# Norm weights moved out of the rows that the experts gather, router logits in column groups, residual on VectorE, biases in four transposes

## The chip, the cores and the metric

One core of a Trainium2 chip runs one launch of the program. The metric is the device time of that launch in microseconds. The kernel before took 1209.48 us (median of 3 runs, 1208.46 to 1210.07).

## What is computed

A decoder layer over 256 tokens of 1024 features: a layer norm, a mixer of three groups (a state-space group, sparse attention, memory attention) that one output projection merges, a second layer norm, and a mixture of 32 experts of which each token takes 4. What the change touches, cut from the reference:

```
mix = concat([y_ssd, y_dsa, y_mem], -1) @ w_out[l]
h = layer_norm(ALPHA * h + mix, ln1_g[l], ln1_b[l])
...
logits = h2 @ router_w + router_b
top_val, top_idx = lax.top_k(logits, 4)
gates = softmax(top_val)
...                                    # per expert e, on the tokens that chose it
gu = xb @ w_gu[e] + b_gu[e]
y  = clamped_swiglu(gu) @ w_down[e] + b_down[e]
...
h = layer_norm(ALPHA * h + sum of gates * y, ln2_g[l], ln2_b[l])
```

All data is 32-bit floating point. The weights of the experts are 384 MiB of the 424 MiB (444.75 MB) that are moved.

## The kernel before

The program has two stages. The *trunk* computes everything up to the second norm and the router. The *expert stage* runs through 32 experts, for each eight row blocks of `w_gu` and four of `w_down`, 1 MiB each, loaded once and used once. A token block `tb` is 128 tokens; there are two.

**Buffers and loads.** All weights, of trunk and experts, go through one set of buffers in SBUF. The loads are issued by SyncE (SP) in a fixed order, `load(c)` at line 379, each as soon as its buffer has been given back. Expert weights are therefore loaded while the trunk still computes, as far as the trunk has given buffers back: twenty of them stand in SP's order before the first one that needs a buffer which an expert has used up.

**Order of the work.** Each piece of work is a generator (`g_...`) that says which engine it wants next and how long it expects to hold it. A list scheduler (`run`, line 242) writes the instructions of all engines in one order when the program is built; each engine then runs its own instructions strictly in that order, and waits on semaphores for data of the others. Priorities are given where a task is added (`add(g, prio)`, a lower number first).

**The output projection** (`g_main`, line 1643, name `out`) accumulates `P`, 128 x 1024 in PSUM, for each token block over 16 row blocks of `w_out`. It begins with two matmuls that put `ALPHA * H` into `P`, by a scaled identity `alphaI` (lines 294 and 1670). Eight row blocks use exact 32-bit matmuls on `yhi`; the other eight, with `shi` and `slo`, use three products of operands that are split into a high and a low part (`w`: split on ScalarE and VectorE, lines 1569 and 1582). The last eight row blocks are done for token block 0, then for token block 1.

**Between the projection and the experts** (`g_ln1`, `g_route`, lines 1142 to 1227), for each token block: ScalarE copies `P` to `res`; VectorE takes mean and variance, a reciprocal root in ten small steps (`rsqrt`), and applies the norm with its weights to get `h` (`h1`); TensorE transposes `res` (`tp`), ScalarE copies the transposes (`hT`), TensorE multiplies by the router's weights (`pl`) into 32 rows and transposes back; VectorE makes the logits (`lgr`), picks four (`sel`), TensorE counts positions (`ppos`), VectorE finishes them (`posm`) and the gates. The norm's weights are folded into the router's weights beforehand by `g_fold` (line 529), sixteen matmuls with 32 columns.

**Gathering.** For each pair of experts VectorE builds a one-hot matrix `oh` from `posm`, TensorE multiplies `h` by it (`pg`), ScalarE copies the product to `xg` (line 1306), and `xg` is the stationary operand of the first expert matmul, `P<-raw,xg`. `g_open` (line 1272) lets the experts begin; `g_start` (line 1237) sets the accumulator `H` to `ALPHA * h` plus gates times `b_down`. `g_bias` (line 505) turns `b_gu` round with sixteen transposes from 32 partitions.

`l1` holds `ln1_g` and `ln1_b`, each spread over 128 partitions by a load of 512 KB in the trunk (line 1138).

Of the kernel before, what the change touches and what calls it, by code (L numbers as in the profile page):

```python
# [15 lines left out]
D = 1024  # L16
NE = 32
# [42 lines left out]
def moe_layer(tc, x, mem, ln_in_g, ln_in_b, w_in, conv_w, conv_b, dt_bias, a_log, d_skip, ssd_norm_g,  # L60
# [233 lines left out]
    alphaI = jp  # L294
    V.tensor_scalar(out=alphaI, in0=ident, scalar1=ALPHA, scalar2=None, op0=OP.mult)
# [14 lines left out]
    free["t8"] += [(0.0, (trunk, f"t8x_{i}", 2048)) for i in range(T8 - T8R)]  # L310

# [112 lines left out]
    bgr = t8([NE, 2 * D], "bgr")  # L424
# [78 lines left out]
    gbT = trunk.tile([128, 16], F32, name="gbT")  # L503

    def g_bias():
        yield after("bgr")
        for q in range(2):
            yield "T", 0.5, "mp"
            pv = take("mp", [128, 8, 64], "pbg")
            for f in range(8):  # L510
                o = q * 1024 + f // 2 * 256 + f % 2
                T.transpose(pv[:, f, :NE], bgr[:, o:o + 255:2], ident[:NE, :NE])
            yield "A", 0.4
            A.copy(out=bgT[:, q * 8:q * 8 + 8, :], in_=pv[:, :, :NE])
            give(pv)
# [13 lines left out]
    def g_fold():  # L529

        yield "T", 1.5, "mp"
# [601 lines left out]
    def g_l1():  # L1133
        yield after("dsa00", "dsa01", "dsa10", "dsa11", "mem0", "mem1")
        yield lambda: min((f[0] for f in free["t8"] if f[1][0] is trunk), default=None)
        l1 = t8([128, 2, D], "l1")
        for i, src in enumerate((ln1_g, ln1_b)):
            nc.sync.dma_start(out=l1[:, i, :], in_=_bcast(src, D))
        L1["g"], L1["b"] = l1[:, 0, :], l1[:, 1, :]
        finish_at("l1")  # L1140
# [24 lines left out]

    def g_route(r, tb, mv, rs):
        hT1 = trunk.tile([128, 8, 128], F32, name="hT1", tag=("vtok", "bc")[tb])
        lgr = trunk.tile([128, 40], F32, name="lgr", tag=f"lgr{tb}")
# [11 lines left out]
        yield "T", 1.8, "mp"  # L1180
# [14 lines left out]
        m8 = trunk.tile([128, 8], F32, name="m8r", tag=f"m8r{tb}")  # L1195
        nm = trunk.tile([128, 1], F32, name="nmr", tag=f"nmr{tb}")
# [5 lines left out]
        add(g_gate(lgr, m8, nm, tb), 8)  # L1202
# [6 lines left out]
        mm(p[:, :NE], supper, sel[:, tb, :], start=tb == 0, stop=True)  # L1209
        yield "V", 0.2  # L1210
# [5 lines left out]
    def g_gate(lgr, m8, nm, tb):  # L1216
# [5 lines left out]
        gs = trunk.tile([128, 1], F32, name="gs", tag=f"gs{tb}")  # L1222
# [14 lines left out]
    def g_start():  # L1237
# [9 lines left out]
        bd = take("bd", [NE, D], "bd")  # L1247
        G.dma_start(out=bd, in_=b_down[0])
        yield "W", 8.0
        yield after(LATE)  # L1250
        for tb in range(2):
# [4 lines left out]
            gT = take("sg", [NE, 128], "gT")  # L1256
            A.copy(out=gT, in_=p[:NE, :128])
            give(p)
            for hf in range(2):
# [5 lines left out]
                V.scalar_tensor_tensor(out=H[:, tb, cs], in0=L1["h1"][:, tb, cs], scalar=ALPHA, in1=p, op0=OP.mult,  # L1265
                                       op1=OP.add)
# [4 lines left out]

    def g_open():

        yield after("pos0", "pos1", "h100", "h101", "h110", "h111", "gate0", "gate1")
# [10 lines left out]
        add(g_start(), 9)  # L1285
        add(g_l2())
# [8 lines left out]
    def gather(oh, xg, n, q):  # L1295
# [9 lines left out]
        yield "A", 0.6  # L1305
        A.copy(out=xg[:, :n, q * 4:q * 4 + 4, :], in_=pv[:, :, :n, :].rearrange("p j e s -> p e j s"))  # L1306
# [292 lines left out]
    def begin(name):  # L1599
# [27 lines left out]
        if name == "out":  # L1627
            add(g_l1())
# [14 lines left out]
    def g_main():  # L1643
# [8 lines left out]
        for i, tb in units:  # L1652
# [31 lines left out]
            for j, (w, r) in enumerate(prods):  # L1684
                for c0, d0, wid in wd:
                    mm(Pt[tb][:, d0:d0 + wid], w, r[:, c0:c0 + wid], start=k == 0 and j == 0 and name != "out",
                       stop=last and j == len(prods) - 1)
            if tb:
# [3 lines left out]
                else:  # L1692
                    used_up(c, o)
            if last:
# [3 lines left out]
                if tb and name == "out":  # L1698
                    give(*Y.values())
# [151 lines left out]
```

## Time and profile before

| What | Value |
|---|---|
| Time, median of 3 runs | 1209.48 us |
| Profiled execution, its own time | 1209.03 us |
| Its span, first to last instruction | 1207.2 us |
| TensorE (PE) busy | 1125.4 us, 93% |
| VectorE (DVE) busy | 369.1 us, 31% |
| ScalarE (ACT) busy | 276.2 us, 23% |
| Moved by DMA | 444.75 MB, 368 GB/s over the span |

The span's start is 0 in all times below. The output projection's last matmul starts at 250.7 us, the first expert matmul at 271.2 us. Engines are named PE, PEld (the weight loads of PE), DVE, ACT, POOL and SP as the profile does. An exact 32-bit matmul stands in the trace as two instructions, so that `x16` can be eight matmuls. An operand's buffer number is left out of its name; `two`, `raw` and `w` are weight buffers and scratch.

### The profile page before, as it was taken

How to read it: one execution, taken by the hardware profiler on the slowest of the kernel's cores; microseconds unless marked ns; L12 is line 12 of the kernel's file. 1: busy time of each engine (PE TensorE's matmuls, PEld its weight loads, DVE VectorE, ACT ScalarE, POOL GpSimd, SP SyncE). 2: the span in 40 equal slices, each digit the busy share in tenths (PEclk: the TensorE clock that was granted, in tenths of full speed). 3: DMA queues.
4: the chain of work that ended last, by engine and by line, in shares of the span. 5: the costliest groups of instructions: out<-in, count | busy, mean ns of one | idle time of the engine just before them, and what ended most of it. 6: DMA issues, size and time to landing. Idle time of an engine off the chain costs nothing. (4 is left out here: it accounts for less than half of the span.)

```text
span 1207.2 us, 13744 instructions
## 1 busy us (share of the span) xinstructions
PE 1125.4 (93%) x5491; PEld 536.1 (44%) x5491; DVE 369.1 (31%) x864; ACT 276.2 (23%) x583; POOL 8.4 (1%) x21
## 2 busy tenths in 40 slices
PE   7999999989999999999998989898989898989894
PEld 5777785774343434434343424242424242424231
DVE  6579667751222211212112111212121112111124
ACT  3576894311111111111111111111111111111110
POOL 1000000000000000000000000000000000000000
PEclk9999999989999999999999999999999999999997
DMA  8845345699999999999999999999999999999993
GB/s 282 280 147 201 105 158 226 231 366 375 422 421 422 422 420 422 422 422 421 422 422 422 421 422 421 422 423 420 422 421 422 423 420 423 420 422 422 421 421 139
DMA packets 71653, 444.75 MB, mean 368 GB/s; under 512 B 9669, under 2 KB 11089, under 8 KB 22145
## 3 DMA queue, kind: packets, MB, share of 16 engines
q1 hardware_dynamic: 70896, 441.43, 89.7%
q0 software_dynamic: 688, 2.39, 0.6%
q8 instruction: 45, 0.74, 0.3%
q14 instruction: 24, 0.19, 0.0%
HBM read 442.73 MB, written 1.06 MB: 368 GB/s over the span
## 5 line engine op out<-in xcount | busy, mean ns | idle before, releaser
L80 PE MATMUL P<-raw,xg 128*64 128x512 f32 x2048 | 464.1, 597 | 33.9 <-DMA raw<-in_w_gu_dram 33.8
L80 PEld LDWEIGHTS P<-raw,xg 128*64 128x64 f32 x2048 | 139.1, 136 | 328.3 <-issue 233.3
L80 PE MATMUL P<-raw,aT 128*64 128x512 f32 x1024 | 238.2, 598 | 12.4 <-DMA raw<-in_w_down_dram 11.2
L1370 DVE TENSOR_TENSOR gb<-tp,bgT 128x512 f32<-128x512 f32 x64 | 44.0, 687 | 574.7 <-PE tp L1366 574.7
L80 PEld LDWEIGHTS P<-raw,aT 128*64 128x64 f32 x1024 | 68.8, 136 | 153.7 <-issue 105.0
L1388 ACT COPY ps<-P 128x512 f32<-128x512 f32 x64 | 34.5, 589 | 416.6 <-PE P L80 416.6
L1425 DVE TENSOR_TENSOR H<-H,psc 128x512 f32<-128x512 f32 x68 | 43.7, 684 | 160.0 <-PE psc L80 160.0
L80 PE MATMUL P<-w,hhi 128*128 128x512 f32 (+1 forms) x288 | 82.2, 401 | 2.1 <-DVE w L1582 2.1
L80 PEld LDWEIGHTS pg<-oh,h 128*128 128x128 f32 x512 | 61.8, 197 | 23.6 <-issue 11.4
L80 PE MATMUL pg<-oh,h 128*128 128x128 f32 x512 | 67.9, 288 | 1.3 <-DVE oh L1292 1.3
L80 PE MATMUL psc<-ye,oht 64*128 64x512 f32 x256 | 63.9, 616 | 0.8 <-ACT ye L1430 0.8
L80 PEld LDWEIGHTS P<-w,hhi 128*128 128x128 f32 x288 | 52.3, 189 | 13.4 <-DVE w L1582 3.0
L1430 ACT ACTIVATE ye<-P,oht 128x512 f32<-128x512 f32 x32 | 22.0, 687 | 124.0 <-PE P L80 124.0
L1377 ACT ACTIVATE sg<-gb 128x256 f32<-128x256 f32 x64 | 26.7, 417 | 96.7 <-DVE gb L1373 96.7
L1306 ACT COPY xg<-pg 128x512 f32<-128x512 f32 x32 | 18.7, 586 | 127.9 <-PE pg L80 127.9
L80 PE MATMUL P<-w,hlo 128*128 128x512 f32 (+1 forms) x144 | 45.7, 390 | 0.0
L1366 PEld LDWEIGHTS tp<-ident,ps 128*128 128x128 f32 x256 | 33.2, 209 | 25.2 <-ACT ps L1388 21.9
L1366 PE MATMUL tp<-ident,ps 128*128 128x128 f32 x256 | 39.2, 296 | 0.0
L1582 DVE TENSOR_TENSOR w<-two,w 128x1024 fp32r<-128x1024 f32 (+2 forms) x28 | 31.3, 1135 | 20.1 <-ACT w L1569 19.8
L1582 DVE TENSOR_TENSOR w<-raw,w 128x1024 fp32r<-128x1024 f32 (+2 forms) x28 | 31.6, 1142 | 18.0 <-ACT w L1569 17.3
L80 PEld LDWEIGHTS psc<-ye,oht 64*128 64x128 f32 x256 | 21.9, 186 | 31.1 <-issue 28.4
L1569 ACT CAST w<-raw 128x1024 fp32r<-128x1024 f32 (+2 forms) x28 | 26.9, 982 | 16.6 <-PE P L80 9.3
(295 smaller groups left out, 788.0 us busy)
## 6 DMA issues: line engine op xcount, KB each, us to landing
raw<-in_w_gu_dram SPq DMA_DIRECT2D x256, 1024.0 KB, 19.8
raw<-in_w_down_dram SPq DMA_DIRECT2D x128, 1024.0 KB, 19.8
two<-in_w_in_dram SPq DMA_DIRECT2D x16, 512.0 KB, 3.8
raw<-in_w_in_dram SPq DMA_DIRECT2D x6, 1024.0 KB, 6.5
two<-in_w_out_dram SPq DMA_DIRECT2D x8, 512.0 KB, 4.0
raw<-in_w_out_dram SPq DMA_DIRECT2D x4, 1024.0 KB, 5.4
LT<-scr_d POOLq DMA_DIRECT2D x2, 1024.0 KB, 6.0
two<-in_w_in_dram SPq DMA_DIRECT2D x6, 264.0 KB, 6.5
```

The source lines that it names most:

```text
L80: T.matmul(o, lhsT=l, rhs=r, start=start, stop=stop)
L1306: A.copy(out=xg[:, :n, q * 4:q * 4 + 4, :], in_=pv[:, :, :n, :].rearrange("p j e s -> p e j s"))
L1366: T.transpose(pv[:, f, :], ps[:, o:o + 255:2], ident)
L1370: V.tensor_tensor(out=gb, in0=pv.rearrange("p f (c s) -> p f c s", c=2), in1=bcol(half).to_broadcast([128, 4, 2, SLOTS]), op=OP.add)
L1377: A.activation(out=sg, in_=gb[:, :, 0, :], func=AF.Sigmoid, scale=1.702)
L1388: A.copy(out=ps[:, c * 512:c * 512 + 512], in_=P[:, c * 512:c * 512 + 512])
L1425: V.tensor_tensor(out=H[:, tb, cs], in0=H[:, tb, cs], in1=ps[hf], op=OP.add)
L1430: A.mul(out=ye, in_=Q[:, :512], mul=oht[:, 256:257])
L1569: A.copy(out=parts[i][0][0], in_=raw_of[c][o])
L1582: V.tensor_tensor(out=lo, in0=raw_of[c][o], in1=hi.bitcast(F32), op=OP.subtract)
```

## The change

- `alphaI` and the four matmuls with it go. `g_ln1` makes `res` with `scalar_tensor_tensor` on VectorE, `ALPHA * H + P`, in two halves; the two copies on ScalarE go. The last row block's matmuls are ordered by halves of the columns.
- The norm's weights are no longer applied before the gather: `h1` is `(res - mean) * rs`, made by two `activation` instructions on ScalarE for each token block. The weights go in when `pg` is evacuated to `xg`: four `activation` instructions with per-partition scale and bias in place of one copy.
- The residual's `ln1_g` is multiplied in later by `g_resid`, in the middle of the expert stage, with a load of `ln1_g` spread over partitions; `ln1_b` comes in as a 33rd row of the matmul with `b_down`. The loads of `l1` in the trunk go.
- Router logits: the eight matmuls write to four groups of 32 rows, and a matmul with `four` (four identities on top of one another) adds the groups. Token block 0's routing has priority 5 in place of 8, token block 1's -1 in place of 0.
- `g_fold` does its sums on VectorE and one matmul in place of sixteen.
- `b_gu` is loaded in four parts on 128 partitions and turned by four transposes in place of sixteen.
- `warm(n)` adds matmuls whose results nobody reads: 8 at the start, 9 and 5 in token block 1's routing.
- Gates are no longer waited for by `g_open`, but by `g_back` and by the load of `b_down`.

The diff, cut to its core:

```diff
-    alphaI = jp
-    V.tensor_scalar(out=alphaI, in0=ident, scalar1=ALPHA, scalar2=None, op0=OP.mult)
+    four, fs = jp[:, 0:NE], jp[:, NE:3 * NE].rearrange("p (c e) -> p c e", c=2)
...
+    def warm(n):
+        t = take("mp", [128, 512], "warm")
+        for i in range(n):
+            mm(t[:, i % 4 * 128:i % 4 * 128 + 128], ident, ident)
+        give(t)
+    warm(8)
...
     def g_bias():
-        for q in range(2):
-            for f in range(8):
-                T.transpose(pv[:, f, :NE], bgr[:, o:o + 255:2], ident[:NE, :NE])
+        for f in range(4):
+            T.transpose(pv[:, f, :], bgr[:, o:o + 255:2], ident)
...
     def g_fold():
-        for k in range(8):
-            mm(p[:, :NE], gbT[:, 8 + k:9 + k].to_broadcast([128, 128]), rw[:, k, :], start=k == 0, stop=k == 7)
...
-        for k in range(8):
-            mm(p[:, NE:2 * NE], ones, rw[:, k, :], start=k == 0, stop=k == 7)
+        V.tensor_tensor(out=t, in0=rw, in1=by(gbT[:, 8:16]), op=OP.mult)
+        V.tensor_reduce(out=fs[:, 0, :], in_=t.rearrange("p k e -> p e k"), axis=AX.X, op=OP.add)
+        V.tensor_tensor(out=rw, in0=rw, in1=by(gbT[:, 0:8]), op=OP.mult)
+        V.tensor_reduce(out=fs[:, 1, :], in_=rw.rearrange("p k e -> p e k"), axis=AX.X, op=OP.add)
+        mm(p[:, :2 * NE], ones, jp[:, NE:3 * NE])
...
     def g_ln1(P, tb):
-            A.copy(out=r[:, cs], in_=P[:, cs])
+            V.scalar_tensor_tensor(out=r[:, cs], in0=H[:, tb, cs], scalar=ALPHA, in1=P[:, cs], op0=OP.mult, op1=OP.add)
-        add(g_route(r, tb, mv, rs), 0 if tb else 8)
+        add(g_route(r, tb, mv, rs), -1 if tb else 5)
-        V.scalar_tensor_tensor(out=H[:, tb, :], in0=r, scalar=mv[:, 0:1], in1=L1["g"], op0=OP.subtract, op1=OP.mult)
+        V.tensor_scalar(out=nm, in0=mv[:, 0:1], scalar1=rs, scalar2=-1.0, op0=OP.mult, op1=OP.mult)
-            V.scalar_tensor_tensor(out=L1["h1"][:, tb, cs], in0=H[:, tb, cs], scalar=rs, in1=L1["b"][:, cs], op0=OP.mult,
-                                   op1=OP.add)
+            A.activation(out=L1["h1"][:, tb, cs], in_=r[:, cs], func=AF.Identity, scale=rs, bias=nm)
...
     def g_route(r, tb, mv, rs):
-            mm(pl[:NE, :128], rw[:, k, :], hT1[:, k, :], start=k == 0, stop=k == 7)
+            q = k % 4 * 32
+            mm(pl[q:q + 32, :128], rw[:, k, :], hT1[:, k, :], start=k < 4, stop=k >= 4)
-        T.transpose(pl[:, 256:256 + NE], lgT, ident[:NE, :NE])
+        mm(pl[:, 256:256 + NE], lgT, four)
+        if tb:
+            warm(9)
...
+        if tb:
+            warm(5)
...
+    def g_resid():
+        yield after("start1", "aT201")
+        nc.sync.dma_start(out=g, in_=_bcast(ln1_g, D))
+                V.scalar_tensor_tensor(out=t, in0=L1["h1"][:, tb, cs], scalar=ALPHA, in1=g[:, cs], op0=OP.mult, op1=OP.mult)
+                V.tensor_tensor(out=H[:, tb, cs], in0=H[:, tb, cs], in1=t, op=OP.add)
...
     def gather(oh, xg, n, q):
-        A.copy(out=xg[:, :n, q * 4:q * 4 + 4, :], in_=pv[:, :, :n, :].rearrange("p j e s -> p e j s"))
+        for j in range(4):
+            A.activation(out=xg[:, :n, k, :], in_=pv[:, j, :n, :], func=AF.Identity, scale=gbT[:, k:k + 1],
+                         bias=gbT[:, 8 + k:9 + k])
...
     def g_main():
-                if name == "out":
-                    for c0 in (0, 512):
-                        mm(Pt[tb][:, c0:c0 + 512], alphaI, H[:, tb, c0:c0 + 512], stop=False)
+            if last:
+                steps.sort(key=lambda x: x[1])
```

**What moves on PE, where token block 1's part of the output projection begins.** Before, its row blocks (`P<-w,shi` and `P<-w,slo`, six instructions each) follow one another:

```order
L80 MATMUL P<-w_2556,shi 128x512 x4
L80 MATMUL P<-w_2556,slo 128x512 x2
L80 MATMUL P<-w_2087,shi 128x512 x4
L80 MATMUL P<-w_2087,slo 128x512 x2
L80 MATMUL P<-w_2115,shi 128x512 x4
L80 MATMUL P<-w_2115,slo 128x512 x2
```

Now token block 0's routing stands between them (`tp` is the transposes of `res`, `pl` the logits, `pl<-jp` the sum over the four groups):

```order
L80 MATMUL P<-w_2525,slo 128x512
L80 MATMUL P<-w_2097,shi 128x512 x4
L80 MATMUL P<-w_2097,slo 128x512 x2
L472 MATMUL tp<-ident,res 128x128 x8
L80 MATMUL P<-w_2121,shi 128x512 x4
L80 MATMUL P<-w_2121,slo 128x512 x2
L80 MATMUL pl<-hT_2619,rw 32x128 x8
L80 MATMUL P<-w_2197,shi 128x512 x4
L80 MATMUL P<-w_2197,slo 128x512 x2
L80 MATMUL pl<-jp,hT_2619 128x32
L80 MATMUL P<-w_2471,shi 128x512 x4
L80 MATMUL P<-w_2471,slo 128x512 x2
```

Half of the routing's work on PE has moved ahead of the projection's end.

**On PE, from the end of the projection to the first expert matmul.** Before, both token blocks are routed here:

```order
L80 MATMUL P<-w_2556,slo 128x512 x2
L459 MATMUL tp<-ident,res 128x128 x16
L80 MATMUL pl<-hT_2636,rw 32x128 x8
L80 MATMUL pl<-hT_2763,rw 32x128 x8
L1188 MATMUL pl<-ident,hT_2636 128x32
L1188 MATMUL pl<-ident,hT_2763 128x32
L80 MATMUL ppos<-sel,ones 128x32
L80 MATMUL ppos<-sel,supper 128x32 x2
L80 MATMUL pcn<-sel,one 1x32 x2
L80 MATMUL pg<-oh,h_2693 128x128 x8
```

Now token block 1 alone, with the matmuls that nobody reads:

```order
L80 MATMUL P<-w_2525,slo 128x512
L472 MATMUL tp<-ident,res 128x128 x8
L80 MATMUL pl<-hT_2785,rw 32x128 x8
L80 MATMUL pl<-jp,hT_2785 128x32
L80 MATMUL warm<-ident 128x128 x9
L80 MATMUL ppos<-sel,ones 128x32
L80 MATMUL ppos<-sel,supper 128x32
L80 MATMUL warm<-ident 128x128 x5
L80 MATMUL pcn<-sel,one 1x32 x2
L80 MATMUL pg<-oh,h_2771 128x128 x8
```

The nine `warm` stand where PE waits for `sel`, the five where it waits for `oh`.

**On DVE, from token block 1's reciprocal root to the first one-hot matrix.** Before, two large operations for `h` and both blocks' choices stand here, and the gates stand ahead of `oh`:

```order
L121 SCALAR_TENSOR_TENSOR ln_rs<-rs_t,rs_u 128x1
L1156 SCALAR_TENSOR_TENSOR H<-res,ln_mv,l_2528 128x1024
L1162 SCALAR_TENSOR_TENSOR h_2693<-H,ln_rs,l_2528 128x512 x2
L1191 SCALAR_TENSOR_TENSOR lgr<-rnc,ln_mv,pl 128x32
L1193 SCALAR_TENSOR_TENSOR lgr<-lgr,ln_rs,rb 128x32
L1197 MAX m8r<-lgr 128x8
L1198 MEMSET m8r 128x4
L1199 MATCH_REPLACE lr<-m8r,lgr 128x40
L1200 TENSOR_SCALAR sel<-lr 128x32
L1191 SCALAR_TENSOR_TENSOR lgr<-rnc,ln_mv,pl 128x32
```

Now:

```order
L121 SCALAR_TENSOR_TENSOR ln_rs<-rs_t,rs_u 128x1
L1170 TENSOR_SCALAR ln_nm<-ln_mv,ln_rs 128x1
L1209 SCALAR_TENSOR_TENSOR lgr<-rnc,ln_mv,pl 128x32
L1211 SCALAR_TENSOR_TENSOR lgr<-lgr,ln_rs,rb 128x32
L1215 MAX m8r<-lgr 128x8
L1216 MEMSET m8r 128x4
L1217 MATCH_REPLACE lr<-m8r,lgr 128x40
L1218 TENSOR_SCALAR sel<-lr 128x32
L1238 TENSOR_SCALAR nmr<-m8r 128x1
L1231 SCALAR_TENSOR_TENSOR posm<-ppos,sel 128x32
L1332 TENSOR_TENSOR oh<-slot,posm 128x128 x2
L1243 SCALAR_TENSOR_TENSOR gate,gs<-lgr,sel 128x32
```

Nineteen rows of before shrink to ten between the root and `oh`; token block 0's share stands further up, during the projection. SP's order of loads is the same up to the twentieth expert load, without the two of `l1`.

## Rows read from the trace of the kernel before

**Rows 1.** Windows: busy us of each engine (instructions), granted clock, DMA share, GB/s.
```profile
100.00:130.00 30.00, 27.11 (x136) 21.38 (x135) 26.77 (x71) 20.48 (x58) 0.00 (x0) 1.00 0.54 187
179.60:251.00 71.40, 71.40 (x311) 47.71 (x310) 48.98 (x91) 24.07 (x46) 0.00 (x0) 1.00 0.63 244
...
264.00:271.20 7.20, 7.20 (x40) 7.08 (x40) 0.69 (x5) 1.46 (x4) 0.00 (x0) 0.59 0.71 290
...
600.00:1180.00 580.00, 534.19 (x2582) 204.40 (x2578) 105.32 (x258) 75.60 (x173) 0.00 (x0) 1.00 1.01 422
```

**Rows 2.** Windows around the last two gaps in the weight stream.
```profile
228.00:236.00 8.00, 8.00 (x49) 6.90 (x48) 7.53 (x9) 3.56 (x5) 0.00 (x0) 1.00 0.30 114
236.00:268.00 32.00, 26.65 (x145) 22.88 (x143) 17.12 (x68) 5.92 (x15) 0.51 (x1) 0.87 1.00 404
268.00:276.00 8.00, 8.00 (x45) 4.74 (x46) 0.00 (x0) 1.28 (x3) 0.00 (x0) 0.88 0.33 116
```

**Rows 3.** SP's waits, 225 to 236 us: in total, times, longest.
```profile
SPq L395 <- DVE w L1582: 10.3, 2, 8.2
```

**Rows 4.** SP timeline: start, duration, instruction, count.
```profile
233.34 15.18 SPq L395 DMA_DIRECT2D raw<-in_w_gu_dram  x9
...
273.15 12.34 SPq L395 DMA_DIRECT2D raw<-in_w_gu_dram  x8
```

**Rows 5.** PE timeline, what the change removes in the trunk, and its neighbours.
```profile
42.21 1.14 PE L512 MATMUL pbg<-ident,bgr 32*128 32x32 f32 x8 [0.24 <-ACT kT L559]
...
179.63 1.87 PE L80 MATMUL pfold<-rw,gbT 128*128 128x32 f32 x16
...
181.80 1.88 PE L80 MATMUL P<-H,jp 128*128 128x512 f32 x4
183.52 1.88 PE L80 MATMUL P<-two,yhi 128*128 128x512 f32 x4
...
230.45 1.87 PE L80 MATMUL pfold<-rw,ones 128*128 128x32 f32 x16
```

**Rows 6.** PE timeline, from the projection's end into the expert stage.
```profile
250.32 0.63 PE L80 MATMUL P<-w,slo 128*128 128x512 f32 x2
250.79 1.98 PE L459 MATMUL tp<-ident,res 128*128 128x128 f32 x16
252.70 3.68 PE L80 MATMUL pl<-hT,rw 128*32 128x128 f32 x32
...
260.81 0.60 PE L80 MATMUL ppos<-sel,ones 128*128 128x32 f32 x2 [3.79 <-DVE nmr L1218]
...
263.91 3.78 PE L80 MATMUL pg<-oh,h 128*128 128x128 f32 x16 [1.34 <-DVE oh L1292]
...
271.18 15.67 PE L80 MATMUL P<-raw,xg 128*64 128x512 f32 x72
...
290.20 2.03 PE L80 MATMUL pg<-oh,h 128*128 128x128 f32 x16
```

**Rows 7.** DVE timeline of the same stretch.
```profile
250.52 1.41 DVE L1162 SCALAR_TENSOR_TENSOR h<-H,ln_rs,l 128x512 f32<-128x512 f32 x2 [5.33 <-PE P L80]
...
253.18 0.21 DVE L483 BATCH_NORM_AGGREGATE ln_mv<-ln_st 128x2 f32<-128x12 f32 x1
...
255.32 1.28 DVE L1156 SCALAR_TENSOR_TENSOR H<-res,ln_mv,l 128x1024 f32<-128x1024 f32 x1
...
257.97 0.24 DVE L1191 SCALAR_TENSOR_TENSOR lgr<-rnc,ln_mv,pl 128x32 f32<-128x32 f32 x1
...
259.27 0.24 DVE L1191 SCALAR_TENSOR_TENSOR lgr<-rnc,ln_mv,pl 128x32 f32<-128x32 f32 x1
...
263.57 0.48 DVE L1292 TENSOR_TENSOR oh<-slot,posm 128x128 f32<-128x128 f32 x2
```

**Rows 8.** Page, DMA issues: size, us from issue to landing.
```profile
raw<-in_w_gu_dram SPq DMA_DIRECT2D x256, 1024.0 KB, 19.8
...
l<-in_ln_g_dram SPq DMA_DIRECT2D x1, 512.0 KB, 4.3
```

More of the change, by code (lines that the diff above doesn't have):

```diff
@@ L293, in moe_layer @@
     V.memset(one, 1.0)
-    alphaI = jp
-    V.tensor_scalar(out=alphaI, in0=ident, scalar1=ALPHA, scalar2=None, op0=OP.mult)
+    four, fs = jp[:, 0:NE], jp[:, NE:3 * NE].rearrange("p (c e) -> p c e", c=2)
+    V.tensor_tensor(out=four, in0=ident[:, 0:32], in1=ident[:, 32:64], op=OP.add)
+    for i in (64, 96):
+        V.tensor_tensor(out=four, in0=four, in1=ident[:, i:i + 32], op=OP.add)
     slot = pp.tile([128, SLOTS], F32, name="slot")
@@ L383, in load @@
         one, two = room("load")
+        if one is None and two is None:
+            one, two = has("rk"), has("st", "st")
         big = two is None or one is not None and one <= two
@@ L502, in moe_layer @@
     cvT = trunk.tile([128, 60], F32, name="cvT")
-    gbT = trunk.tile([128, 16], F32, name="gbT")
+    gbT = pp.tile([128, 16], F32, name="gbT")
     def g_bias():
         yield after("bgr")
-        for q in range(2):
-            yield "T", 0.5, "mp"
-            pv = take("mp", [128, 8, 64], "pbg")
-            for f in range(8):
-                o = q * 1024 + f // 2 * 256 + f % 2
-                T.transpose(pv[:, f, :NE], bgr[:, o:o + 255:2], ident[:NE, :NE])
-            yield "A", 0.4
-            A.copy(out=bgT[:, q * 8:q * 8 + 8, :], in_=pv[:, :, :NE])
-            give(pv)
+        yield "T", 0.45, "mp"
+        pv = take("mp", [128, 4, 128], "pbg")
+        for f in range(4):
+            o = f // 2 * 256 + f % 2
+            T.transpose(pv[:, f, :], bgr[:, o:o + 255:2], ident)
+        yield "A", 0.6
+        A.copy(out=bgT.rearrange("p (q f) e -> p f q e", q=4), in_=pv.rearrange("p f (q e) -> p f q e", q=4))
+        give(pv)
         give(bgr)
@@ L1131, in moe_layer @@
     posm = pp.tile([128, 2, NE], F32, name="posm")
[L1133 to L1140, printed above, removed]
     def g_ln1(P, tb):
@@ L1172, in g_route @@
         for b0 in (0, 4):
+            yield after(f"res{tb}{b0 // 4}")
             yield "T", 0.45, "mp"
@@ L1221, in g_gate @@
         yield "V", 0.58
-        gs = trunk.tile([128, 1], F32, name="gs", tag=f"gs{tb}")
+        gs = sm.tile([128, 1], F32, name="gs", tag=f"gs{tb}", bufs=1)
         V.scalar_tensor_tensor(out=gate[:, tb, :], in0=lgr[:, :NE], scalar=1.0, in1=sel[:, tb, :],
@@ L1246, in g_start @@
         give(pcn)
-        bd = take("bd", [NE, D], "bd")
-        G.dma_start(out=bd, in_=b_down[0])
+        yield after("gate0", "gate1")
+        bd = take("bd", [NE + 1, D], "bd")
+        G.dma_start(out=bd[:NE, :], in_=b_down[0])
+        G.dma_start(out=bd[NE:NE + 1, :], in_=ln1_b)
         yield "W", 8.0
@@ L1255, in g_start @@
             yield "A", 0.2, "sg"
-            gT = take("sg", [NE, 128], "gT")
-            A.copy(out=gT, in_=p[:NE, :128])
+            gT = take("sg", [NE + 1, 128], "gT")
+            G.memset(gT[NE:NE + 1, :], ALPHA)
+            A.copy(out=gT[:NE, :], in_=p[:NE, :128])
             give(p)
@@ L1270, in g_start @@
         finish_at("start1")
+    def g_resid():
+        yield after("start1", "aT201")
+        yield lambda: has("t4")
+        g = take("t4", [128, D], "l1")
+        nc.sync.dma_start(out=g, in_=_bcast(ln1_g, D))
+        yield "W", 6.0
+        for tb in range(2):
+            for hf in range(2):
+                cs = slice(hf * 512, hf * 512 + 512)
+                yield "V", 1.4, "ye"
+                t = take("ye", [128, 512], "t")
+                V.scalar_tensor_tensor(out=t, in0=L1["h1"][:, tb, cs], scalar=ALPHA, in1=g[:, cs], op0=OP.mult, op1=OP.mult)
+                V.tensor_tensor(out=H[:, tb, cs], in0=H[:, tb, cs], in1=t, op=OP.add)
+                give(t)
+        give(g)
     def g_open():
-        yield after("pos0", "pos1", "h100", "h101", "h110", "h111", "gate0", "gate1")
+        yield after("pos0", "pos1", "h100", "h101", "h110", "h111")
         trunk.release()
@@ L1285, in g_open @@
         add(g_start(), 9)
+        add(g_resid(), 9)
         add(g_l2())
@@ L1526, in g_load @@
             if c == SIDE:
-                nc.sync.dma_start(out=bgr, in_=b_gu[0])
+                for q in range(4):
+                    nc.sync.dma_start(out=bgr[q * NE:q * NE + NE, :], in_=b_gu[0, :, q * 512:q * 512 + 512])
                 dma[0] += 0.75
@@ L1683, in g_main @@
                 prods = [(l, hi), (l, lo), (m, hi)]
-            for j, (w, r) in enumerate(prods):
-                for c0, d0, wid in wd:
-                    mm(Pt[tb][:, d0:d0 + wid], w, r[:, c0:c0 + wid], start=k == 0 and j == 0 and name != "out",
+            steps = [(j, w) for j in range(len(prods)) for w in wd]
+            if last:
+                steps.sort(key=lambda x: x[1])
+            for j, (c0, d0, wid) in steps:
+                    w, r = prods[j]
+                    mm(Pt[tb][:, d0:d0 + wid], w, r[:, c0:c0 + wid], start=k == 0 and j == 0,
                        stop=last and j == len(prods) - 1)
@@ L1693, in g_main @@
                     used_up(c, o)
+            if name == "out" and k == 7 and tb:
+                give(*Y.values())
             if last:
@@ L1697, in g_main @@
                     give(mhi, mlo)
-                if tb and name == "out":
-                    give(*Y.values())
         yield after("experts")
```

64 lines of the change are left out of this document (37 added, 27 removed).

## The prediction, made before the changed kernel ran

> **What bounds the kernel now.** I read the windows first. Over 580 us of the expert stage the DMA share is 1.01 at 422 GB/s, while PE is busy 534.19 of 580 and DVE and ACT far less [rows 1]: the weight stream bounds this stage, and 1 MiB costs 2.48 us (1,048,576 bytes by 422 GB/s). Work taken from an engine there is worth nothing by itself. What counts is when the stream can begin to run without a break, how long it breaks afterwards, and how many bytes it carries; the stretch behind the last load is not touched by the change.
>
> Then the windows around 230 and 270 us. The share is 0.30 in 228 to 236 and 0.33 in 268 to 276, with 1.00 between them [rows 2]. So the stream stands still twice for 8 x 0.70 = 5.6 us and 8 x 0.67 = 5.4 us. SP's waits name what ended the first gap: a buffer given back by VectorE's split of the output projection (`DVE w L1582`, up to 8.2 us) [rows 3]; the load then goes out at 233.34 [rows 4]. The second gap ends when the first expert matmul, which starts at 271.18 [rows 6], gives a buffer back: the next load goes out at 273.15 [rows 4]. From 179.6 to 251.0 PE is busy 71.40 of 71.40 at clock 1.00 [rows 1], so PE paces the end of the trunk, and with it the split buffers behind the first gap.
>
> So the time before is the start of the last stretch, plus the second gap, plus a stream of fixed length, plus a tail.
>
> **The change part by part.** *A. The start of the last stretch.* From PE ahead of it go:
> - the first `pfold`: 1.87 us for 16 [rows 5]. A group's listed time has some 0.16 us of overlap with the next (four `P<-H,jp` are listed with 1.88, the next starts 1.72 later), so 1.7;
> - the four `P<-H,jp`, which are two such groups, one for each token block: 2 x 1.72 = 3.4 [rows 5];
> - twelve of sixteen bias transposes: two groups of 1.14 [rows 5] become four transposes, 0.5 at the 0.12 of one `tp` instruction (1.98 over 16) [rows 6], which leaves 1.8. These lie early, and between 100 and 130 PE idles 2.9 of 30 us with DVE at 26.77 [rows 1], so part of it can be lost to a DVE wait. Ends 0 and 1.8; I take half, 0.9.
>
> Given back: the new `pfold` matmul (0.2, two instructions of 0.12 [rows 5]) and a delay of the splits behind the fold's four operations on DVE. One costs at most 0.70, as a 128x512 half of `h` does [rows 7]; DVE is free 0.47 of the window before the first gap [rows 2], but 22 of 71 us over the whole stretch [rows 1]. Ends 0 and 2.8; I take 0.4, near the free end. A = -1.7 - 3.4 - 0.9 + 0.2 + 0.4 = **-5.4** (ends -6.7 and -2.1).
>
> *B. The second gap.* It closes if the first expert matmul, W, moves earlier by as much as the stream's pause moves plus the gap itself: 5.4 (A) + 5.4, less 0.8 (C, below) = 10.0 us. How far does W move?
>
> First the projection's end. -5.4 as in A, -1.7 for the second `pfold` [rows 5], which stands behind the first gap, +2.4 for token block 0's routing, which now stands between row blocks: half of `tp` 1.0 [rows 6], logits 0.9, sum over the groups 0.2, `ppos` 0.3 (half of 0.60 [rows 6]); +0.3 for its handovers. Together -4.4. The logits: `pl` is 3.68 for both blocks [rows 6], 1.84 for one. Four groups of 32 columns are not in the trace, two are: a `P<-raw,xg` instruction of 512 columns takes 15.67/72 = 0.22 [rows 6], a `P<-two,yhi` one 1.72/4 = 0.43 [rows 5]. That is a factor of two; I take it, 0.9. Ends 0.45 and 1.84.
>
> Then from the projection's end to W. Before: 250.95 (250.32 + 0.63) to 271.18 [rows 6], 20.2 us. After, counted from the projection's end:
> - mean, variance and root as before, 255.32 - 250.95 = 4.4 [rows 7]: VectorE's second half of `res` (0.70, as `h`) takes the place of ScalarE's copy;
> - the small `nm`, 0.2. The 1.28 of `H` and the 1.41 of `h`, which stood here [rows 7], are gone;
> - logits and choice of one block in place of two, 259.27 - 257.97 = 1.3 [rows 7]: 5.9;
> - `ppos`, `posm` and handovers 0.9, `oh` 0.48 [rows 7]: 7.3, and 0.5 for the `warm` and `pcn` matmuls ahead of `pg`: 7.8;
> - `pg` to W. Before, 263.91 to 271.18, 7.3 us, with PE busy throughout but at clock 0.59 [rows 1, 6]. It had waited 3.79 and 1.34 shortly before [rows 6], and falls behind such idling; at full clock `pg` takes 2.03 in place of 3.78 [rows 6]. With one block fewer to wait for and 14 matmuls in the two waits I expect the high clock: 7.3 x 0.59 = 4.3, or two `pg` and one us for the rest, 5.1. I take 5.1: 12.9.
>
> So W moves by -4.4 - (20.2 - 12.9) = -11.7, to 259.5; the margin over 10.0 is 1.7 us and the gap closes: B = **-5.4** (ends -5.4 and 0). Every us by which W is later than that margin costs one.
>
> A drain of TensorE belongs here. The column groups stand twice among 128-wide matmuls. The trace has that switch already: `pg` at 290.20, behind column-group matmuls, takes 2.03 for 16, and `tp` without a switch 1.98 [rows 6]; 0.05 us is within what I can read, and four switches stay inside the margin. The Trainium skill, TensorEngine Tiling (Array Packing), section "Key Properties", says that changing the tiling mode drains the TensorE. It gives no price; by that rule W is later at each of the four switches by the time the array takes to empty, which could only raise the chance of the second rival.
>
> *C.* Block 0's routing on PE between block 1's row blocks (2.4 us) delays the buffers of the last row blocks, and with them loads that the stream wants then. The stream carries 1.00 there [rows 2], with several loads in flight, so most of it is covered. Ends 0 and 2.4; I take **+0.8**.
>
> *D. Bytes.* `g_resid` puts a load of 512 KB for `ln1_g` into the full stream: 524,288 bytes at 422 GB/s, **+1.2** (ends 0 and 4.3, the landing time of such a load [rows 8]). The two trunk loads that go ahead of a gap give nothing back.
>
> *At nothing:* four ScalarE operations for one in each `xg`, since ACT is busy 75.60 of 580, and `g_resid`'s eight halves of at most 0.7 on DVE, busy 105.32 of 580 [rows 1]; both lie beside the stream. If that cover went, `xg` would be late for an expert, a fraction of a us for each pair, which PE's 46 idle us take up. The 8 `warm` at the start and the 33rd row of `b_down` cost PE a us in all, in idle time.
>
> **Sum.** -5.4 - 5.4 + 0.8 + 1.2 = -8.8, against the profiled execution's 1209.03: 1200.2. The median of the runs shown, 1209.48, is 0.45 above it, so I forecast **1200.6**, in its own range 1198 to 1203.
>
> **The rivals.**
> 1. *The start of the last stretch is not PE's to give.* What released SP is a split on DVE [rows 3], and DVE is busy 7.53 of 8 in that window [rows 2], so DVE may pace the splits. Against it: PE shows no idle time for 71 us [rows 1]. A shrinks to -1.5, the gap still closes: -1.5 - 5.4 + 0.8 + 1.2 = -4.9, 1204.6.
> 2. *W is late.* The clock falls all the same (for: 0.59 in the window before W [rows 1]) and `pg` to W keeps 7.3 in place of 5.1, and the norm's chain is 2.5 longer than I count: 4.7 late, less the margin of 1.7, leaves a gap of 3.0: 1203.7. Against: the removed DVE work is read directly from rows.
> 3. *More is gained.* All of the bias transposes' time survives and the fold delays nothing (A -6.7), C and D hide in what is left of gaps: -6.7 - 5.4 = -12.1, 1197.4. For: the stream's pauses have room; against: DVE's load around 100 to 130.
> 4. *Slower.* SP issues loads strictly in order, so `ln1_g`'s load, in the middle of the expert stage, waits for its buffer and all weight loads queue behind it. Some eight loads are in flight (19.8 us from issue to landing [rows 8], 2.48 each), so up to 19.8 us cost nothing; beyond that each us is lost in full. To eat the gain of 8.8 and 2.4 more, it must wait over 19.8 + 8.8 + 2.4 = 31 us; then 1212 or more. Against: a buffer comes free every 2.5 us.
> 5. *It does nothing that can be measured*: trunk and stream re-arrange so that the pause only moves: about 1209.
>
> **How the numbers follow.** The forecast has 0.50, the rivals 0.17, 0.13, 0.12, 0.04 and 0.04. From 1195 to 1206.5 lie nearly all of the forecast and most of rivals 1 to 3, 0.8 together. A measurement of this kernel tells about 0.2%, 2.4 us, from no change. Faster by more: the forecast and rivals 1 to 3, less 0.04 for their late tails, 0.88; within it: rival 5 and 0.03 of those tails, 0.07; slower: rival 4 and 0.01, 0.05.
>
> **What would show it.** A: SP's first expert load behind the first gap goes out at 228 in place of 233.3. B: the first `P<-raw,xg` starts at 259.5, the clock in `pg` before it is 1.00, and a window of 8 us around it has a DMA share of 1.0. C: no break above 1 us between. D: the load of `ln1_g` lands without a break in the share. The prediction is wrong in A if DVE is what PE waits for before 228, in B if a gap stays while W comes after 261.2, and in its whole frame if the DMA share falls below 1 in the expert stage.

## The result, and the profile after

The changed kernel took 1201.28 us (median of 4 runs, 1199.58 to 1202.75), the kernel before 1209.77 beside it; the ratio is 0.993 (95% interval 0.9915 to 0.9946). Forecast were 1200.6 us, from 1195 to 1206.5. The profiled execution took 1199.58 us against 1209.03, 9.45 less. The time came out as forecast; the terms did not, and two large errors among them cancel.

The windows of the changed kernel, in the columns of [rows 1]:

```profile
179.60:251.00 71.40, 69.61 (x326) 45.68 (x326) 53.66 (x120) 26.83 (x53) 1.00 (x2) 1.00 0.72 285
228.00:236.00 8.00, 8.00 (x44) 6.39 (x46) 6.00 (x14) 1.67 (x3) 0.00 (x0) 1.00 0.99 405
236.00:258.00 22.00, 20.27 (x154) 16.57 (x153) 10.64 (x56) 7.54 (x17) 0.00 (x0) 1.00 1.01 421
258.00:264.00 6.00, 6.00 (x31) 2.21 (x31) 0.00 (x0) 1.50 (x4) 0.00 (x0) 1.00 0.58 214
264.00:276.00 12.00, 12.00 (x65) 5.12 (x62) 0.00 (x0) 1.47 (x4) 0.00 (x0) 1.00 1.02 416
...
840.00:880.00 40.00, 4.65 (x32) 3.01 (x30) 2.65 (x4) 1.77 (x5) 0.00 (x0) 0.59 1.01 422
880.00:895.00 15.00, 14.23 (x64) 7.10 (x66) 5.19 (x9) 1.51 (x4) 0.00 (x0) 0.85 0.81 315
```

Against [rows 2]: the share in 228 to 236 rose from 0.30 to 0.99, and the gap around 271 became one of 6 x 0.42 = 2.5 us around 260. New is a break of 15 x 0.19 = 2.9 us at 880 to 895, after 40 us in which PE did nearly nothing.

SP's loads (start, duration, instruction, count), where [rows 4] had 233.34 and 273.15:

```profile
224.76 17.30 SPq L408 DMA_DIRECT2D raw<-in_w_gu_dram  x9
243.11 3.56 SPq L408 DMA_DIRECT2D raw<-in_w_down_dram  x4
260.40 12.35 SPq L408 DMA_DIRECT2D raw<-in_w_gu_dram  x8
```

And PE. The kernel before had the first `P<-w,shi` at 225.48, which the rows ahead of the prediction did not show:

```profile
225.48 1.49 PE L80 MATMUL P<-w,shi 128*128 128x512 f32 x4
```

The changed kernel, where [rows 6] had the projection's end at 250.95 and the first expert matmul at 271.18:

```profile
219.79 1.49 PE L80 MATMUL P<-w,shi 128*128 128x512 f32 x4
...
235.89 0.65 PE L80 MATMUL pl<-hT,rw 128*32 128x128 f32 x16
236.46 1.20 PE L80 MATMUL P<-w,shi 128*128 128x512 f32 x4
...
245.45 0.39 PE L80 MATMUL P<-w,slo 128*128 128x512 f32 x1
246.62 1.31 PE L472 MATMUL tp<-ident,res 128*128 128x128 f32 x8 [0.78 <-DVE res L1154]
...
249.72 2.25 PE L80 MATMUL warm<-ident 128*128 128x128 f32 x18
...
252.49 1.36 PE L80 MATMUL warm<-ident 128*128 128x128 f32 x10
253.78 0.28 PE L80 MATMUL pcn<-sel,one 128*1 128x32 f32 x4
253.99 2.05 PE L80 MATMUL pg<-oh,h 128*128 128x128 f32 x16
...
256.46 2.03 PE L80 MATMUL pg<-oh,h 128*128 128x128 f32 x16
258.42 15.67 PE L80 MATMUL P<-raw,xg 128*64 128x512 f32 x72
```

The projection ends at 245.84 (245.45 + 0.39), the first expert matmul, W, starts at 258.42, and 2.0 us later its buffer starts the stream again. `pg` takes 2.05 at full clock, in place of 3.78.

The break at 880, in the waits from 820 to 900 us (in total, times, longest), then on SP and DVE, and last in SP's own waits from 868 to 892 us:

```profile
DVE t L1306 <- DMA two<-in_ln_g_dram: 44.7, 1, 44.7
PEld pg L80 <- DVE H L1468: 37.0, 1, 37.0
PE pg L80 <- DVE H L1468: 36.1, 1, 36.1
```

```profile
858.61 0.33 SPq L1299 DMA_DIRECT2D two<-in_ln_g_dram  x1
861.10 5.30 SPq L408 DMA_DIRECT2D raw<-in_w_gu_dram  x3
868.56 21.85 SPq L408 DMA_DIRECT2D raw<-in_w_down_dram  x4
```

```profile
877.25 0.69 DVE L1306 SCALAR_TENSOR_TENSOR t<-h,two 128x512 f32<-128x512 f32 x1 [44.66 <-DMA two<-in_ln_g_dram]
```

```profile
SPq L408 <- DMA two<-in_ln_g_dram: 8.3, 1, 8.3
SPq L408 <- PE P L80: 7.4, 3, 4.7
SPq L408 <- DVE t L1306: 6.0, 1, 6.0
```

In order of time: `g_resid`'s load of `ln1_g` goes out at 858.6, behind the loads already in flight, and lands 18.6 us later. VectorE, strictly in order, stood at the first use of it 44.7 us, from 832.6 to 877.25; 26 of these had passed before the load went out. Behind that use stands `H`, which PE needs before the next `pg`, so PE stood 36.1 us as well. The stream broke on SP: `ln1_g` lies in half of a weight buffer (`two`, line 1298 of the changed kernel), the fifth weight load behind it takes that buffer, and SP, in order too, waited for it 14.3 us, 8.3 until `ln1_g` had landed and 6.0 until VectorE's last use of it. That load went out at 883.27, and the one after it waited 4.7 us for a buffer from PE.

### The profile page after: what moved, and what is told of

The parts are those of the page before. It is cut to its first block, busy times and chain, and to the rows that moved or that the text cites. A ratio compares the mean times of both kernels' runs of the same rounds, so it can differ in the third digit from the quotient of the medians.

```text
span 1197.8 us, 13864 instructions
## 1 busy us (share of the span) xinstructions
PE 1110.0 (93%) x5487; PEld 533.9 (45%) x5487; DVE 373.8 (31%) x877; ACT 305.5 (26%) x678; POOL 9.3 (1%) x24
## 5 line engine op out<-in xcount | busy, mean ns | idle before, releaser
L80 PE MATMUL P<-raw,xg 128*64 128x512 f32 x2048 | 458.3, 595 | 14.9 <-DMA raw<-in_w_gu_dram 14.9
L80 PEld LDWEIGHTS P<-raw,xg 128*64 128x64 f32 x2048 | 141.5, 137 | 299.3 <-issue 253.2
L80 PE MATMUL P<-raw,aT 128*64 128x512 f32 x1024 | 235.8, 597 | 6.7 <-DMA raw<-in_w_down_dram 6.7
L80 PE MATMUL pg<-oh,h 128*128 128x128 f32 x512 | 67.4, 286 | 36.1 <-DVE H L1468 36.1
L1348 ACT ACTIVATE xg<-pg,gbT 128x128 f32<-128x128 f32 x128 | 48.2, 456 | 149.9 <-PE pg L80 149.9
L1409 PEld LDWEIGHTS tp<-ident,ps 128*128 128x128 f32 x256 | 33.1, 208 | 25.2 <-ACT ps L1431 22.7
L1613 ACT CAST w<-raw 128x1024 fp32r<-128x1024 f32 (+2 forms) x28 | 26.8, 984 | 16.1 <-PE P L80 10.6
## 6 DMA issues: line engine op xcount, KB each, us to landing
raw<-in_w_gu_dram SPq DMA_DIRECT2D x256, 1024.0 KB, 19.8
raw<-in_w_down_dram SPq DMA_DIRECT2D x128, 1024.0 KB, 19.8
```

The source lines that it names most:

```text
L80: T.matmul(o, lhsT=l, rhs=r, start=start, stop=stop)
L1348: A.activation(out=xg[:, :n, k, :], in_=pv[:, j, :n, :], func=AF.Identity, scale=gbT[:, k:k + 1], bias=gbT[:, 8 + k:9 + k])
L1409: T.transpose(pv[:, f, :], ps[:, o:o + 255:2], ident)
L1613: A.copy(out=parts[i][0][0], in_=raw_of[c][o])
```

## Experiments

Executions of one kernel differ by some 2 us already where the trunk ends (the eighth load of the changed kernel goes out at 224.13, 224.76 and 226.51), so each profile is also read in two stretches: from the eighth expert load (the one at 224.76 above) to W, and from the load that W releases (260.40) to the load of `ln2_g` near the end. All times are from SP's and PE's timelines; the median is of the timed runs.

| Kernel | 8th load | W | between | released load | `ln2_g` | between | median us, ratio to before |
|---|---|---|---|---|---|---|---|
| before | 233.34 | 271.18 | 37.84 | 273.15 | 1168.89 | 895.74 | 1209.77 |
| changed | 224.76 | 258.42 | 33.66 | 260.40 | 1159.35 | 898.95 | 1201.28, 0.993 |
| after_again | 224.13 | 257.81 | 33.68 | 259.78 | 1159.50 | 899.72 | 1200.48, 0.9936 (0.9923 to 0.995) |
| after_3 | 226.51 | 260.20 | 33.69 | 262.18 | 1161.39 | 899.21 | 1201.45, 0.9936 (0.9923 to 0.995) |
| late_use | 225.22 | 258.89 | 33.67 | 260.87 | 1158.55 | 897.68 | 1199.3, 0.9923 (0.991 to 0.9936) |
| no_resid | 225.86 | 259.49 | 33.63 | 261.47 | 1157.65 | 896.18 | 1197.5, 0.9903 (0.9888 to 0.9917) |
| late8 | 228.05 | 258.77 | 30.72 | 260.75 | 1159.87 | 899.12 | 1200.41, 0.9933 (0.9919 to 0.9946) |
| late_w | 224.11 | 261.30 | 37.19 | 263.28 | 1163.16 | 899.88 | 1203.72, 0.9961 (0.9947 to 0.9974) |
| one_group | 225.43 | 261.23 | 35.80 | 263.20 | 1161.82 | 898.62 | 1203.54, 0.9955 (0.994 to 0.9969) |
| no_warm | 226.39 | 261.67 | 35.28 | 263.64 | 1162.32 | 898.68 | 1200.6, 0.9927 (0.9914 to 0.9941) |
| no_warm_2 | 225.95 | 261.02 | 35.07 | 263.00 | 1161.55 | 898.55 | 1201.61, 0.9939 (0.9925 to 0.9952) |
| best | 223.96 | 256.98 | 33.02 | 258.96 | 1156.99 | 898.03 | 1198.57, 0.9917 (0.9903 to 0.9931) |
| best_row | 224.83 | 257.82 | 32.99 | 259.80 | 1156.37 | 896.57 | 1195.63, 0.9887 (0.9872 to 0.9903) |

Theory: as long as a gap is left before it, W alone sets when the stream runs again; the start of the stretch ahead of it then counts for nothing. And the expert stage lost 3.2 us, to the bytes of `ln1_g` and to a break, because VectorE waited for it. The rivals: the start of the stretch counts by itself, as my sum added it; the loss is the load's own.

**The changed kernel again.** Two baselines, on two chips: after_again on that of late_use, no_resid and late8, after_3 on that of no_warm_2 and best_row. late_w, one_group, no_warm and best ran on a third, with the kernel before beside them but not the changed one.

> The changed kernel once more, as the baseline on the same chip. Every theory: 1201.3 us, 0.993 of before, as in the four runs so far.

> The changed kernel a third time, as the baseline of this chip job: 1200.5 to 1201.3 us by every theory.

Both within 1 us of what was expected. The medians differ by 1 us, while the 33.7 us between the eighth load and W stay within 0.03 in the three traces.

**late8: the start of the stretch, 3 us later.**

```
+        if what == "load" and loading[0] == NT + 7:
+            return has("rk"), None
         if what == "pair" or loading[0] >= NT:
```

> The eighth expert load takes a buffer of the larger kind, as before the change, and so waits for a later split: the last stretch of the stream should start some 3 us later, near 228.5 in place of 225.5. Theory (the gap of 2.5 us that is left ends when the first expert matmul gives a buffer back, so the first expert matmul at 258.4 sets the time, not the start of the stretch): the gap at 259 to 261.5 shrinks to below 0.5 us, the time rises by no more than 0.6 us. Rival (the start of the stretch sets the time, as my sum added it): 2.9 us more, 1204.2.

Measured: the load goes out at 228.05 in place of 224.76, of the gap near 260 some 0.2 us are left (share 0.97, before this edit 0.58), and the time is that of the baseline (1200.41 to 1200.48). W, not the start of the stretch, sets the time; the rival's 1204.2 is excluded.

```profile
258.00:264.00 6.00, 6.00 (x34) 2.45 (x34) 0.00 (x0) 1.69 (x5) 0.00 (x0) 1.00 0.97 375
```

**late_w: W later.**

```
-            warm(5)
+            warm(21)
```

> Sixteen more matmuls that nobody reads ahead of the first pg (21 in place of 5), 32 instructions, about 3.7 us at 0.12 each, less what PE waited for the one-hot matrix anyway (under 0.3). Theory (the first expert matmul sets the time as long as a gap is left): all of it is lost, 3.4 to 3.7 us more than the changed kernel, 1205; the gap near 260 grows to 6 us. Rival (the margin of 1.7 us of the prediction is there): 1.7 to 2 us more, 1203.

Measured: W 3.5 us later behind the eighth load (37.19 to 33.68), and the stream resumes 1.98 us behind W as before; the share in 258 to 264 is down to 0.09. The time, 1203.72, is 3.2 and 2.3 us above the two baselines, both of other chips; it lies between the 1205 that I expected and the rival's 1203 and decides nothing. The trace does: with a gap already there, there is no margin of 1.7 us.

```profile
258.00:264.00 6.00, 6.00 (x45) 4.17 (x45) 0.00 (x0) 3.28 (x9) 0.00 (x0) 1.00 0.09 37
```

**one_group: the logits in one group.**

```
-            mm(pl[q:q + 32, :128], ..., start=k < 4, stop=k >= 4)
+            mm(pl[:NE, :128], ..., start=k == 0, stop=k == 7)
...
-        mm(pl[:, 256:256 + NE], lgT, four)
+        mm(pl[:, 256:256 + NE], lgT, ident[:NE, :NE])
```

> The logits' eight matmuls go into one group of 32 rows again, with the transpose back, as before the change. The changed kernel's trace has 0.65 us for sixteen instructions in four groups, before had 1.84. Theory: the first expert matmul is later by 1.2 us for token block 1's logits and by some of 1.2 us for token block 0's, which stands in the row blocks ahead of it: 1.5 to 2.4 us, and the time with it, 1203.2. Rival (PE waits for VectorE there, the logits' length is hidden): no change, 1201.3.

Measured: W 2.1 us later, the time 3.1 us above after_again's and 2.1 above after_3's, both of other chips; the intervals hold both. Token block 1's logits are 1.94 us long again. The column groups are worth about 2 us on the path to W.

```profile
250.15 1.94 PE L80 MATMUL pl<-hT,rw 128*32 128x128 f32 x16
```

**no_warm, twice: without the 14 matmuls that nobody reads.**

```
-        if tb:
-            warm(9)
...
-        if tb:
-            warm(5)
```

> The 9 and the 5 matmuls that nobody reads in token block 1's routing go. If they keep the granted clock up, it falls during or after PE's waits, pg takes 3.8 in place of 2.05 as before the change, the first expert matmul is 2 to 3 us later, and the time too, 1203.5 to 1204.5. Rival (one routing less is wait short enough): the clock stays at 1.00, the first expert matmul is where it was or up to 0.3 us earlier, 1201.

> The kernel without the 14 matmuls a second time. In the first trace the clock fell to 0.50 from 256 to 258 us and the first pg took 3.75 us; from the eighth expert load to the first expert matmul it was 35.3 us, in the changed kernel 33.7. Theory (the matmuls keep the clock up): 1.6 us again in the trace, and 1 to 2 us in the time, 1202. Rival (the clock falls in some executions alone): 33.7 us and no change in the time.

Measured, in both traces: PE waits 2.12 us, the granted clock falls to 0.50 (1.2 of 2.4 GHz) before that wait is over, and the first `pg` takes 3.75 us. From no_warm:

```profile
253.00:254.00 1.00, 0.11 (x1) 0.11 (x1) 0.76 (x6) 1.00 (x3) 0.00 (x0) 0.50 1.03 434
...
253.89 0.64 PE L80 MATMUL ppos<-sel,supper 128*128 128x32 f32 x2 [2.12 <-DVE nmr L1234]
...
255.10 3.75 PE L80 MATMUL pg<-oh,h 128*128 128x128 f32 x16 [0.27 <-DVE oh L1328]
```

W is 1.4 to 1.6 us later behind the eighth load, where I first expected 2 to 3. The clock costs about 2 us from `pg` to W (6.57 and 6.36 in place of 4.43), and the 14 matmuls themselves had cost 0.5: without them `pg` starts 28.7 us behind the eighth load, with them 29.2. In the time nothing shows (0.1 and 0.2 us above the baselines, intervals of 1.6 either way), and both of my forecasts for it, 1203.5 to 1204.5 and then 1 to 2 us more, were missed. That speaks against the theory that every us of W is a us of the time, or is scatter; the two stretches of the table together are 0.8 us longer than in the baselines. The clock's part is shown, what it is worth in the end stays open.

**late_use, no_resid: the load of `ln1_g` and who waits for it.**

```
         yield "W", 6.0
+        yield after("aT231")
```

> g_resid's load of ln1_g stays where it is, its eight operations on VectorE come three experts later. Theory (VectorE, in order, waits 44.7 us for the load; PE waits 36.1 us for VectorE; the stream breaks for some 3 us because no buffer comes free): the wait goes, the break in 880 to 895 us goes, 2.5 to 3 us less than the changed kernel, about 1198.5. Rival (the break belongs to the load itself, in SP's strict order and in the queue): the break stays, same as the changed kernel, 1201.3.

no_resid takes out `add(g_resid(), 9)`, so it leaves out the residual of the second norm.

> g_resid is left out, load and VectorE operations (the residual of the second norm is then missing). Theory: break of 3 us and 1.24 us of bytes go, about 1197; so 1 to 1.5 us less than with the operations moved later. Rival: only the bytes and the load's own break go; moving the operations later did nothing and this one gives all of the 4 us.

Measured for late_use: PE's wait of 36.1 us and the break are gone (share in 880 to 895, with PE's busy time ahead of it, below). From the released load to `ln2_g` it takes 897.7 in place of 899.0 to 899.7 us. So the rival, that the load by itself breaks the stream, falls. The size was wrong: 1.6 us against the three baselines' mean of 899.3, where I expected 2.5 to 3, and the medians' intervals overlap. Eight profiles have the early use (898.55 to 899.88, mean 899.1) and two the late one (897.68, and 898.03 in best); by these it is 1.2 us. no_resid takes another 1.5 us off, close to the 1.24 of its bytes, with the scatter of 1.3 us that the eight show.

```profile
840.00:880.00 40.00, 37.65 (x192) 15.46 (x188) 6.37 (x14) 6.63 (x17) 0.00 (x0) 1.00 1.01 421
880.00:895.00 15.00, 12.21 (x56) 4.06 (x56) 4.20 (x12) 1.91 (x4) 0.00 (x0) 1.00 1.02 423
```

late_use changes two things at once: PE no longer stands still, and no weight load wants `ln1_g`'s buffer while it is still in use (SP waits for it 0.9 us at most). The trace of late8 tells them apart. SP's waits from 845 to 915 us there, and the window of the break:

```profile
SPq L410 <- DMA two<-in_ln_g_dram: 10.8, 1, 10.8
SPq L410 <- DVE t L1308: 5.3, 1, 5.3
SPq L410 <- PE P L80: 0.6, 2, 0.3
...
880.00:895.00 15.00, 0.00 (x0) 0.00 (x0) 9.07 (x18) 1.64 (x5) 0.00 (x0) 0.50 0.86 343
```

SP waited 16.1 us for that buffer and never more than 0.3 us for one from PE, and the stream broke all the same, by 15 x 0.14 = 2.1 us, with an expert stage as long as the baselines' (899.12). So a buffer that SP waits for in its order is enough to break the stream. The 4.7 us for PE's buffer in the changed kernel add nothing that can be read in the length of the stage.

**best, best_row: a faster version.** best is late_use with the return way of the first two experts behind the first products:

```
-        yield after(f"oh{e // 2}", "gate0", "gate1", ...)
+        yield after(f"oh{e // 2}", "gate0", "gate1", ..., *(["xg0_1"] if e < 2 else []))
```

> late_use, and the transposes and products for the return way of the first pair of experts (0.6 us on PE) moved behind the first expert matmuls. Theory: 2.5 to 3 us less from the first, and the first expert matmul 0.5 us earlier from the second: 1197.8 to 1198.3, the fastest of all complete versions. Rival: 1198.5 or above, the second edit gives nothing since the evacuation of pg on ScalarE comes last.

best_row also loads `ln1_g` as one row and spreads it by PE, early in the expert stage:

```
-        nc.sync.dma_start(out=g, in_=_bcast(ln1_g, D))
...
+        g = take("bd", [1, D], "bd")
+        G.dma_start(out=g, in_=ln1_g)
...
+        al = take("sg", [1, 128], "gT")
+        G.memset(al, ALPHA)
...
+            mm(p, al, g[:, cs])
...
-                V.scalar_tensor_tensor(out=t, in0=L1["h1"][:, tb, cs], scalar=ALPHA, in1=g[:, cs], op0=OP.mult, op1=OP.mult)
+                V.scalar_tensor_tensor(out=t, in0=L1["h1"][:, tb, cs], scalar=1.0, in1=p, op0=OP.mult, op1=OP.mult)
```

> As the version with the later use and the moved return-way transposes, but ln1_g comes as one row of 4 KB and is spread by two matmuls from one partition; no load of 512 KB in the weight stream, and no half buffer held. Theory (the 512 KB cost what they take in the stream, 1.24 us): 1.2 us less than that version, 1197.3; no break anywhere after 262 us. Rival (such a load hides in the stream's unevenness at the end): the same, 1198.5.

Measured: W 0.7 us earlier behind the eighth load in both, where 0.5 was expected. best's median, 1198.57, is 0.3 us above my range and at the rival's figure, but the rival's reason, that the second edit gives nothing, is not what the trace shows. Between best and best_row the expert stage is 1.5 us shorter (898.03 to 896.57), with no break; the median falls from 1198.57 to 1195.63, about twice what these 1.5 explain and more than the 1.2 I expected. The two ran on different chips, and their intervals only meet (at 0.9903), so the size stays open between 1.5 and 2.9 us. best_row is 0.9887 of before, 1.1% faster, and clear of the changed kernel (0.993, and 0.9936 on the same chip).

## Why the prediction was right, point by point

**Frame.** The stream bounds the expert stage, the tail behind the last load is the same, and only the stream's pauses and bytes count: that held. But by the prediction's own sign the frame is wrong if the share falls below 1 in the expert stage, and it did, once: 0.81 in 880 to 895, with 1.01 on either side (600 to 870, 900 to 1150). What the sum left out there is under D. From the released load on, the differences of the table add up: -12.75 there, +3.2 to `ln2_g`, -9.5 at the end.

**A, the trunk.** -5.4 was forecast for PE ahead of the stretch; the first `P<-w,shi` moved from 225.48 to 219.79, by -5.7. Of the bias transposes' 1.8 us nothing was lost (the same `P<-w,hhi` starts at 122.15 before and 120.23 after, 1.9 us earlier), where I took half; so the other terms of A gave some 0.7 us less than I counted. But the start of the stretch moved by -8.6, 233.34 to 224.76. The step that failed: "SP's order of loads is the same", so the start moves with PE. The order is the same; the buffers are not. In the changed kernel the eighth load's buffer comes free with the split of `two`, in the kernel before with the first of the two splits of `raw` at 232.06. VectorE, before and after:

```profile
229.19 1.22 DVE L1582 TENSOR_TENSOR w<-two,w 128x1024 fp32r<-128x1024 f32 x1
...
232.06 2.35 DVE L1582 TENSOR_TENSOR w<-raw,w 128x1024 fp32r<-128x1024 f32 x2
```

```profile
223.51 1.22 DVE L1626 TENSOR_TENSOR w<-two,w 128x1024 fp32r<-128x1024 f32 x1
```

223.51 + 1.22 = 224.73, and SP goes at 224.76; before, the first of the two ends after half of 2.35, at 233.2, and SP goes at 233.34, while `two` was done at 230.4. These 2.9 us were worth nothing: late8 takes them away and loses nothing.

**B, the second gap.** W was forecast for 259.5 and came at 258.42: -12.8 in place of -11.7, 12.6 us behind the projection's end in place of 12.9. The clock in `pg` was 1.00, as forecast. The gap did not close. With the start 8.6 us earlier W had to move by 8.6 + 5.4 = 14.0 to close it, and moved by 12.8. That leaves 1.2; the other 1.3 of the 2.5 us are C's, below. The sum A + B was nearly right all the same (-11.5 us in pauses against -10.8), because the two are no independent terms. The stream resumes at W or goes on without a break, whichever is later; I should have written one term, the later of the two.

**Logits.** 0.9 us a block was taken, 0.65 came for sixteen instructions (1.84 before), a factor of 2.8. The next matmul, 128 wide, starts at 236.46, within the 0.65 that begin at 235.89: no drain above 0.1 us can be read. The prediction's reading for this was of the wrong row: the `pg` at 290.20 stands behind 128-wide transposes. The one behind column groups is 3.4 us ahead of it and takes 2.05, which changes nothing:

```profile
283.67 3.17 PE L80 MATMUL P<-raw,xg 128*64 128x512 f32 x14
286.78 2.05 PE L80 MATMUL pg<-oh,h 128*128 128x128 f32 x16
```

The Trainium skill, TensorEngine Tiling (Array Packing), section "Key Properties", has changing the mode drain the engine; in this trace that costs less than 0.1 us. The same page of the Trainium skill, section "Theoretical Speedup", gives up to 4x for a dimension of 32 or less; the trace agrees as a bound, with 2.8.

**C, +0.8.** This term had the wrong sign. Breaks of 0.4 and 0.2 us are there, at 226 and 229. But from the eighth load to the released one, less the gap, it is 39.8 - 5.4 = 34.4 us before and 35.6 - 2.5 = 33.1 after, so the stretch is 1.3 us shorter, not longer. A part is a break of the kernel before that is gone: the share in 245 to 250 was 0.92, and is 1.01. Where the rest comes from is not settled. Like A's excess it lay ahead of W and was worth nothing.

**D, +1.2, and "at nothing".** The bytes cost about what was forecast: 1.5 us between late_use and no_resid, and between best and best_row. The step that failed: that `g_resid`'s work on VectorE lies "beside the stream". I looked at how busy VectorE is, and asked neither what stands behind an instruction that waits nor who wants the buffer that it holds. That cost 1.2 to 1.6 us beyond the bytes. The fourth rival had the right place, SP's strict order, and the wrong load: it let `ln1_g`'s load wait for its buffer, and in the trace a weight load waited for `ln1_g`'s. It also held waits of up to 19.8 us to be free; SP's waits of 14.3 us (16.1 in late8) broke the stream by 2.9 us (2.1). Of this break only 1.2 to 1.6 us arrive at the end; where the rest went is not settled.

**The two errors.** The stream's resumption was counted at -10.0 (A, B and C) and came at -12.75, by the pauses -8.6 - 2.9 - 1.3; `g_resid` and the rest of the expert stage were counted at +1.2 and came at +3.2. The sum is -9.5 in place of -8.8. That an error of -2.75 and one of +2.0 all but cancel is luck: the range held, but not because its terms did.

## What to carry to other kernels

A stream of loads with a fixed set of buffers resumes when the first consumer gives one back: before adding up gains ahead of that point and a gap at it, ask which of the two comes last, and count only that. An operation moved "beside" a bound stage is free only if nothing that the stage needs stands behind it on its engine while it waits, and if the stream does not want the buffer that it holds. A load put behind a full queue lands a queue's length after it is issued (here 18.6 us); its use must be placed that much later, and the next load that takes its buffer later still. Small constants needed on all partitions are cheaper as one row spread by a matmul than as half a MiB in a stream that sets the time.

## What the runs showed that I had not expected

PE without work for 36 us cost the kernel under 2 us, since the stream went on from buffers already free and from loads in flight (share 1.01 in 840 to 880). And the eighth expert load goes out anywhere from 223.96 to 226.51 us in executions in which the path from there to W repeats within 0.06 us where it is the same code (33.63 to 33.69 in five). That is most of the spread between runs of one kernel (3.2 us); where in the trunk it arises stays open.
